# Issuing the first small store between tile 0's activations, and computing the last tile in two chunks of 4 rows

## The chip, the cores and the metric

The kernel runs on one core of a Trainium2 chip. The metric is the device time of one execution in microseconds. Every execution has a trace span too, about 2 us shorter than its time.

## The reference

```python
x: float32 [32, 512, 2048]
x1, x2 = x[..., :1024], x[..., 1024:]
out = x1 * (1 / (1 + exp(-x1))) * x2        # float32 [32, 512, 1024]
```

It reads 134.2 MB and writes 67.1 MB, with one activation and one multiply per output element.

## The kernel before

The 16,384 rows are cut into 16 tiles of 128 partitions with K = 8 rows each. A tile's load is 8 MB (64 KB per partition), its store 4 MB (32 KB per partition). There are two input and two output buffers. The activation runs on ScalarE (ACT in the profile), the multiply on VectorE (DVE). Loads are issued by SyncE (SP), stores by ACT; SPq and ACTq mark the instructions that issue them. Tile 0 and the last tile are computed in chunks of 2 rows, the others in one piece. Tile 0 is stored in five transfers of growing size.

```python
K = 8; KC_EDGE = 2; KS = 4
OPENING = [
    (slice(0, None, 4), slice(0, 2)),      # 256 KB: every 4th partition, rows 0 and 1
    (slice(2, None, 4), slice(0, 4)),      # 512 KB
    (slice(2, None, 4), slice(4, None)),   # 512 KB
    (slice(0, None, 4), slice(2, None)),   # 768 KB
    (slice(1, None, 2), slice(None)),      # 2 MB
]
...
load(0); load(1)
for i in range(n_tiles):
    ...
    if i < n_tiles - 1:
        kc = KC_EDGE if i == 0 else K
        for c in range(0, K, kc):
            silu(ot, xt, c, c + kc)        # ACT
            mul(ot, xt, c, c + kc)         # DVE, in place on ot
        for ps, ks in OPENING if i == 0 else [(slice(None), slice(None))]:
            nc.scalar.dma_start(out=ov[ps, ks], in_=ot[ps, ks])
        if i + 2 < n_tiles:
            load(i + 2)                    # waits until the multiply has freed the input buffer
        continue
    for c in range(0, K, KC_EDGE):         # the last tile
        silu(ot, xt, c, c + KC_EDGE)
        if c == K - KC_EDGE:
            nc.scalar.dma_start(out=ov[:, :KS], in_=ot[:, :KS])
        mul(ot, xt, c, c + KC_EDGE)
    nc.scalar.dma_start(out=ov[:, KS:], in_=ot[:, KS:])
```

Of the kernel before, what the change touches and what calls it, by code (L numbers as in the profile page):

```python
# [1 line left out]

# [4 lines left out]


def issue_ahead_of_the_first_barrier(nc):




    head, body = nc.main_func.blocks[:2]
    load = next(ins for ins in body.instructions if type(ins).__name__ == "InstDMACopy")
    at = next(
        j for j, ins in enumerate(head.instructions)
        if ins.engine == load.engine and type(ins).__name__ == "InstDrain"
    )
    body.instructions = [ins for ins in body.instructions if ins.name != load.name]  # L20
    head.instructions = head.instructions[:at] + [load] + head.instructions[at:]


@with_exitstack
def kernel(
    ctx: ExitStack,
    tc: tile.TileContext,
    x: bass.AP,
    out: bass.AP,
):  # L30






    nc = tc.nc
    P = nc.NUM_PARTITIONS

    x_flat = x.flatten_outer_dims()  # L40
    out_flat = out.flatten_outer_dims()
    num_rows, in_cols = x_flat.shape
    half = in_cols // 2
    dt = x_flat.dtype

    K = 8
    KC_EDGE = 2
    KS = 4
    OPENING = [
        (slice(0, None, 4), slice(0, 2)),  # L50
        (slice(2, None, 4), slice(0, 4)),
        (slice(2, None, 4), slice(4, None)),
        (slice(0, None, 4), slice(2, None)),
        (slice(1, None, 2), slice(None)),
    ]
    PLAN = [K] * (num_rows // (P * K))

    in_pool = ctx.enter_context(tc.tile_pool(name="in_pool", bufs=2))
    out_pool = ctx.enter_context(tc.tile_pool(name="out_pool", bufs=2))

    plan = []
    row = 0
    for k in PLAN:
        plan.append((row, k))
        row += P * k
    assert row == num_rows
    n_tiles = len(plan)

    def view(flat, i):
        row0, k = plan[i]  # L70
        return flat[row0:row0 + P * k].rearrange("(p k) d -> p k d", k=k)

    nc.at_finalize(issue_ahead_of_the_first_barrier)


    ctx.enter_context(tc.manual_schedule())

    loaded = {}

    def load(i):  # L80
        xt = in_pool.tile([P, K, in_cols], dt, name="xt")
        nc.sync.dma_start(out=xt[:, :plan[i][1], :], in_=view(x_flat, i))
        loaded[i] = xt

    def silu(ot, xt, c, ce):
        nc.scalar.activation(  # L86
            out=ot[:, c:ce, :],
            in_=xt[:, c:ce, :half],
            func=mybir.ActivationFunctionType.Silu,
        )  # L90

    def mul(ot, xt, c, ce):
        nc.vector.tensor_mul(  # L93
            out=ot[:, c:ce, :],
            in0=ot[:, c:ce, :],
            in1=xt[:, c:ce, half:],
        )

    load(0)
    load(1)  # L100
    for i in range(n_tiles):
        xt = loaded.pop(i)
        ov = view(out_flat, i)
        ot = out_pool.tile([P, K, half], dt, name="ot")
        if i < n_tiles - 1:
            kc = KC_EDGE if i == 0 else K
            for c in range(0, K, kc):
                silu(ot, xt, c, c + kc)
                mul(ot, xt, c, c + kc)

            for ps, ks in OPENING if i == 0 else [(slice(None), slice(None))]:
                nc.scalar.dma_start(out=ov[ps, ks], in_=ot[ps, ks])
            if i + 2 < n_tiles:
                load(i + 2)
            continue

        for c in range(0, K, KC_EDGE):
            silu(ot, xt, c, c + KC_EDGE)
            if c == K - KC_EDGE:
                nc.scalar.dma_start(out=ov[:, :KS], in_=ot[:, :KS])  # L120
            mul(ot, xt, c, c + KC_EDGE)
        nc.scalar.dma_start(out=ov[:, KS:], in_=ot[:, KS:])


# [1 line left out]
_INS = ['x']  # L126
_OUTS = [((32, 512, 1024), 'float32')]


# [23 lines left out]
```

## Time and profile before

| | before |
|---|---|
| time, 3 runs before the change was tried | 470.62 us median (470.6 to 472.49) |
| span of the profiled run | 468.5 us |
| DVE, ACT busy | 30%, 24% |
| HBM traffic over the span | 430 GB/s |
| first packet, last landing | 1.00 us, 467.51 us |

The way to read it is to ask when the DMA engines were not busy. Between the first packet and the last landing they practically always are (share 1.00 from 1 to 467 us, at 432 GB/s). Of the busy shares only this one is near 100% (DVE has 30%, ACT 24%), so the time is set by the queue of transfers, and compute matters only where it lets that queue run empty. The prediction below shows the lines.

### The profile page before, as it was taken

The page shows a single profiled execution, that of the slowest core. Times are in us where ns is not written, and L with a number is a line of the kernel's source. Part 1 is how long each engine was busy: PE and PEld are TensorE (multiplying, and loading weights), DVE is VectorE, ACT ScalarE, POOL GpSimd, SP SyncE. Part 2 cuts the span into 40 slices and gives each one's busy share as a digit, 9 for nine tenths or more (in the row PEclk, how much of TensorE's full clock was granted, in tenths as well). Part 3 has the DMA queues.
Part 4 walks back from the last instruction along what each step waited for, and adds up shares of the span by engine and source line. Part 5 has one row for each costly group of instructions (what it writes and reads, how often), then busy time and mean ns, then how long its engine had stood idle before and what let it go on. Part 6 is the DMA issues. An engine that isn't in the chain of part 4 may idle for free.

```text
span 468.5 us, 189 instructions
## 1 busy us (share of the span) xinstructions
DVE 139.5 (30%) x22; ACT 114.3 (24%) x23; POOL 0.2 (0%) x4
## 2 busy tenths in 40 slices
DVE  0070600704207052070510606116060150602551
ACT  1142305005050140601406023060230603206060
POOL 0000000000000000000000000000000000000000
DMA  9999999999999999999999999899999899999998
GB/s 425 397 453 425 448 403 403 492 403 403 448 487 408 403 448 414 481 403 425 425 448 448 403 448 492 358 448 448 431 464 448 380 425 492 403 448 403 448 403 359
DMA packets 4881, 201.34 MB, mean 430 GB/s; under 512 B 592, under 2 KB 592, under 8 KB 592
## 3 DMA queue, kind: packets, MB, share of 16 engines
q1 hardware_dynamic: 2304, 134.22, 66.4%
q10 hardware_dynamic: 2576, 67.11, 33.2%
q14 instruction: 1, 0.01, 0.0%
HBM read 134.22 MB, written 67.11 MB: 430 GB/s over the span
## 4 chain that ended last, share of the span: by engine, by line
DMA 72%; DVE 14%; ACT 11%; DVEq 0%; issue 0%
DMA out_dram<-ot 63%; DVE ot L93 14%; ACT ot L86 11%; DMA xt<-in_x_dram 9%; DVEq L148 0%
## 5 line engine op out<-in xcount | busy, mean ns | idle before, releaser
L93 DVE TENSOR_TENSOR ot<-ot,xt 128x8192 f32<-128x8192 f32 (+1 forms) x22 | 139.5, 6363 | 319.2 <-ACT ot L86 319.2
L86 ACT ACTIVATE ot<-xt 128x8192 f32<-128x8192 f32 (+1 forms) x22 | 113.0, 5163 | 340.1 <-DMA out_dram<-ot 306.1
L86 ACT ACT_TABLE_LOAD x1 | 1.3, 1283 | 0.8 <-PEq L137 0.8
L137 POOL MEMSET const-bfloat16-1.0<- 128x1 bf16 x1 | 0.1, 103 | 0.0
L137 POOL MEMSET const-uint8-127<- 128x1 uint8 x1 | 0.1, 102 | 0.0
L137 POOL MEMSET const-float32-0.0<- 128x1 f32 x1 | 0.1, 100 | 0.2 <-issue 0.2
L137 POOL MEMSET const-float32-1.0<- 128x1 f32 x1 | 0.1, 99 | 0.0
## 6 DMA issues: line engine op xcount, KB each, us to landing
out_dram<-ot ACTq DMA_DIRECT2D x14, 4096.0 KB, 42.2
out_dram<-ot ACTq DMA_DIRECT2D x3, 2048.0 KB, 8.8
out_dram<-ot ACTq DMA_DIRECT2D x2, 512.0 KB, 17.1
out_dram<-ot ACTq DMA_DIRECT2D x1, 768.0 KB, 27.9
xt<-in_x_dram SPq DMA_DIRECT2D x16, 35.1
out_dram<-ot ACTq DMA_DIRECT2D x1, 256.0 KB, 10.8
```

The costliest lines, as they stand in the source:

```text
L86: nc.scalar.activation(out=ot[:, c:ce, :], in_=xt[:, c:ce, :half], func=mybir.ActivationFunctionType.Silu,)
L93: nc.vector.tensor_mul(out=ot[:, c:ce, :], in0=ot[:, c:ce, :], in1=xt[:, c:ce, half:],)
L137: nc = _bacc.Bacc("TRN2", target_bir_lowering=False, num_devices=1)
```

## The change

At the head, the first of the five small stores is meant to go out earlier, from between tile 0's activations rather than behind all four. At the tail, the last tile is computed in two large chunks rather than four small ones, and its two stores stand behind both multiplies, each waiting for its own half only (in the profile after, the first is issued at 457.25, the second multiply ends at 461.55).

```diff
-            for c in range(0, K, kc):
+            parts = list(OPENING) if i == 0 else [(slice(None), slice(None))]
+            for n, c in enumerate(range(0, K, kc)):
                 silu(ot, xt, c, c + kc)
+
+                if n == 1:
+                    ps, ks = parts.pop(0)
+                    nc.scalar.dma_start(out=ov[ps, ks], in_=ot[ps, ks])
                 mul(ot, xt, c, c + kc)
-
-            for ps, ks in OPENING if i == 0 else [(slice(None), slice(None))]:
+            for ps, ks in parts:
                 nc.scalar.dma_start(out=ov[ps, ks], in_=ot[ps, ks])
 ...
-        for c in range(0, K, KC_EDGE):
-            silu(ot, xt, c, c + KC_EDGE)
-            if c == K - KC_EDGE:
-                nc.scalar.dma_start(out=ov[:, :KS], in_=ot[:, :KS])
-            mul(ot, xt, c, c + KC_EDGE)
-        nc.scalar.dma_start(out=ov[:, KS:], in_=ot[:, KS:])
+        for c in range(0, K, KS):
+            silu(ot, xt, c, c + KS)
+            mul(ot, xt, c, c + KS)
+        for c in range(0, K, KS):
+            nc.scalar.dma_start(out=ov[:, c:c + KS], in_=ot[:, c:c + KS])
```

## The prediction

> **What bounds the kernel now.** I read the page first (busy shares and the chain), then the busy time by stretch of the span, then the timeline of the two ends, since the change touches only tile 0 and the last of the 16 tiles. The page:
>
> ```profile
> span 468.5 us, 189 instructions
> DVE 139.5 (30%) x22; ACT 114.3 (24%) x23; POOL 0.2 (0%) x4
> ...
> HBM read 134.22 MB, written 67.11 MB: 430 GB/s over the span
> ...
> DMA 72%; DVE 14%; ACT 11%; DVEq 0%; issue 0%
> ```
>
> No compute engine is busy a third of the time; 72% of the chain that ended last is DMA. The chain also shows 25% of DVE and ACT, which would be misleading: a chain names what released each step, not which resource was full. Whether the DMA engines ever ran dry is told by the stretches (columns: stretch, length, DVE, ACT and POOL busy with counts, clock, DMA share, GB/s):
>
> ```profile
> 0.00:1.00 1.00, 0.00 (x0) 0.23 (x1) 0.20 (x4) 1.00 0.00 0
> 1.00:22.00 21.00, 0.00 (x0) 1.18 (x2) 0.00 (x0) 1.00 1.07 449
> 22.00:44.00 22.00, 8.90 (x4) 7.78 (x5) 0.00 (x0) 1.00 0.98 417
> ...
> 120.00:410.00 290.00, 86.92 (x11) 70.29 (x10) 0.00 (x0) 1.00 1.00 434
> 410.00:448.00 38.00, 9.15 (x2) 7.14 (x2) 0.00 (x0) 1.00 0.99 428
> 448.00:458.00 10.00, 8.17 (x4) 7.20 (x4) 0.00 (x0) 1.00 0.97 419
> 458.00:467.00 9.00, 0.73 (x1) 0.00 (x0) 0.00 (x0) 1.00 0.96 409
> 467.00:468.50 1.50, 0.00 (x0) 0.00 (x0) 0.00 (x0) 1.00 0.00 0
> ```
>
> A packet is counted whole where it starts, so a single short stretch can be off by a packet (the 1.07 is that). The reader is to see that all 16 engines move data from 1.0 us to about 467 us, at both ends too. The kernel is a queue of 201.33 MB: at 434 GB/s of the long stretch that is 463.9 us; add 1.0 us before the first packet and 1.5 us after the last (closing work), and 466.4 of 468.5 us are accounted for. **About 2 us** are all that any reordering can win, 0.4%. The time is some 2.1 us over the span (470.62 against 468.5).
>
> **The two ends.** The timeline (start us, length us, engine, line, operation):
>
> ```profile
> 21.87 5.51 ACT L86 ACTIVATE ot<-xt 128x2048 f32<-128x2048 f32 x3 [19.82 <-DMA xt<-in_x_dram]
> 23.81 8.90 DVE L93 TENSOR_TENSOR ot<-ot,xt 128x2048 f32<-128x2048 f32 x4 [23.81 <-ACT ot L86]
> 26.14 0.56 ACTq L112 DMA_DIRECT2D out_dram<-ot  x1
> 27.29 1.89 ACT L86 ACTIVATE ot<-xt 128x2048 f32<-128x2048 f32 x1
> 28.34 6.23 ACTq L112 DMA_DIRECT2D out_dram<-ot  x4
> ...
> 447.89 7.31 ACT L86 ACTIVATE ot<-xt 128x2048 f32<-128x2048 f32 x4 [17.17 <-DMA out_dram<-ot]
> 449.83 8.90 DVE L93 TENSOR_TENSOR ot<-ot,xt 128x2048 f32<-128x2048 f32 x4 [10.39 <-ACT ot L86]
> 454.36 0.34 ACTq L120 DMA_DIRECT2D out_dram<-ot  x1
> 458.76 0.34 ACTq L122 DMA_DIRECT2D out_dram<-ot  x1
> ```
>
> At the head, the first store stands in the program behind all four activations, yet it was issued at 26.14, before the fourth started at 27.29[...]. The first multiply ran 23.81 to 26.11, so the store left 0.03 us after the data it needs. At the tail, the store of tile 14 (issued 439.47, landed 18.0 us later, at 457.5) is still draining when the last tile's first half is issued at 454.36.
>
> [...] the packet records have tile 15's first 16 KB packets right behind tile 14's last packet on each engine. [...] The rows by shape (1897 ns for 2048, 7029 ns for 8192) give (7029 - 1897)/6144 = 0.835 ns and 186 ns[...].
>
> **Head, step by step.** Removed: nothing. Moved: the 256 KB store, from behind activation 4 to between activation 2 and multiply 2. It depends on multiply 1, as before, so it still can't leave before 26.11: issue at 26.14, gain 0. The cost is new: activation 3 now stands behind it. Before, activation 3 started at 25.49; now ACT's sequencer waits until 26.11, issues for 0.56 us (to 26.70), and activation 3 starts near 26.75, 1.26 us late. It ends at 26.75 + 1.90 = 28.65. Multiply 2 ran until 28.31, so multiply 3 starts at 28.67 instead of 28.23, and multiply 4 with it ends at about 33.2 instead of 32.71: **+0.45 us**. On that end hang stores 3 to 5 and load 2, all issued 0.45 us later. Neither is on the path: load 1 lands only at 43.4, so load 2 queues behind 10 us of transfers, and store 2 (issued 28.34, unchanged, landing 43.6) is ahead of stores 3 to 5 in ACT's queue. What the change buys at the head is 0, what it costs is hidden.
>
> **Tail, step by step.** Removed: two activations and two multiplies of 2048 columns per partition, as four of each become two of 4096. From the shapes, an activation of 4096 takes 186 + 4096 x 0.835 = 3.61 us. For the multiply: (8693 - 2286)/6144 = 1.043 ns and 150 ns, so 150 + 4271 = 4.42 us. With the same start, 447.89: activation 1 ends at 451.50, multiply 1 runs 451.52 to 455.94, activation 2 ends near 455.1, multiply 2 runs to about 460.3. The first-half store is issued at 455.96 instead of 454.36 (**1.6 us later**), the second at 460.35 instead of 458.76 (1.6 us later). The coarser chunk saves a little fixed cost and loses the overlap of ACT and DVE, 1.7 us of fill.
>
> Does that reach the end? Tile 14's last packets end per engine between 456.83 and 457.17 (packet records). Before, the first-half store was there 2.5 us ahead of need. Now it has 0.9 to 1.2 us. From an issue to the first packet, the only measurement on an idle queue is the first load: issued at 0.0, packets from 1.00 to 1.80 us depending on the engine. The same for a store gives first packets at 456.96 to 457.76 against a need at 456.83 to 457.17: a bubble of 0 to 0.9 us, **0.4 us** as an estimate. Then 2 MB takes 8 packets of 0.607 us = 4.86 us per engine, to about 462.3; the second half, issued at 460.35, has its packets ready by 461.4 to 462.2, so no second bubble. Last data then lands at 467.5 + 0.4.
>
> **Sum.** Head 0, steady tiles 0 (their instructions and transfers are the same, and the share is 1.00), tail +0.4: span 468.9, time 470.62 + 0.4 = 471.0 us.
>
> **The rivals.**
> 1. The intent works: the first store starts earlier, so the transfers mix sooner and tile 2 gets its buffer sooner. For: tile 2's activation does wait for stores to land (14 such waits, 306.1 us). Against: the store was not stuck, and the engines are full, so even an earlier store only swaps the order of packets. It would make 470.1 to 470.6; the 2 us not accounted for cap it at 468.6.
> 2. The tail's delay shows in full: 1.6 us later stores end the program 1.6 us later, 472.2. For: nothing else is left to do after them. Against: it needs tile 14's store to have ended before 454.4, and it ends at 457.5, which absorbs 2.5 us less the start-up of a transfer.
> 3. The tail's delay is hidden altogether: start-up for a store that follows on a running queue may be under 0.9 us [...]. Then 470.6, no change. This is nearly as likely as my 0.4.
> 4. The held activation 3 disturbs the steady rhythm. If the 0.45 us late load 2 opened a gap, 471.1 alone, 471.5 with the tail. Against: load 1 has 10 us left at that time.
>
> **Range and chances.** Rivals 1 to 4 span 470.1 to 472.2. The runs of the kernel before alone span 470.6 to 472.49, and a median of few runs could catch such a high one, so the range is 470.1 to 472.3, with its middle above the prediction. A change of over 2% means 9.4 us: faster is ruled out by the 2 us that are there to win (0.005 for what I can't see), slower would need the engines to idle for 9 us, which no step comes near (0.01). Within 2%: 0.985.
>
> **What would show each step right or wrong.** Head: the first store's issue stays at 26.1, with activation 3 near 26.75 instead of 25.49, and the fourth multiply ends near 33.2; an issue well before 26 would refute the working. Load 1 still lands near 43.4, and the steady stretch stays at 434 GB/s. Tail: two activations of 3.6 us and two multiplies of 4.4 us, stores issued 8.1 and 12.5 us after the last tile's first activation, and the DMA share between 456 and 458 us a little lower. The prediction is wrong if the last tile's first activation starts more than 0.5 us off 447.9, or if the span moves by over 1.5 us.

That 434 GB/s is all that the 16 engines can move, which the "about 2 us" presume, is not shown; it is the rate of the 290 us from 120 to 410. That a waiting store holds back what stands behind it on ACT, on which the +0.45 us rest, was an assumption until the profile after showed it (store issued from 26.21 to 26.76, third activation at 26.81). Why a store that stands behind four activations is issued before the fourth starts is not shown. The packet records at the tail, in numbers: on each of the 16 engines tile 15's first 16 KB packet starts 0.002 us after tile 14's last packet ends (456.838 after 456.836 on the first, 457.171 after 457.169 on the last).

## The result and the profile after

The changed kernel took 470.46 us (median of 6 runs, 470.3 to 471.49). The kernel before, in 6 runs (the three above and three beside the changed kernel), took 471.23 us (470.6 to 472.49). The ratio is 0.9984, 95% interval 0.9966 to 1.0002: the same at the 2% mark. Ratios here are the mean time of one kernel's fast runs over the mean of the other's in the same call, so they are not quite the ratio of the medians quoted. Executions over 1.5% slower than the fastest of the same kernel are left out of the means.

The execution that was profiled happens to be the slowest of the six, 471.49 us. From its page:

```profile
span 469.6 us, 185 instructions
DVE 139.4 (30%) x20; ACT 114.2 (24%) x21; POOL 0.2 (0%) x4
...
DMA 72%; DVE 14%; ACT 11%; DVEq 1%; issue 0%
```

There are four instructions fewer, and the shares are those of before. The busy time by stretch (stretch, length, DVE, ACT and POOL busy with counts, clock, DMA share, GB/s):

```profile
120.00:410.00 290.00, 86.92 (x11) 70.29 (x10) 0.00 (x0) 1.00 1.00 434
...
448.00:457.00 9.00, 4.21 (x1) 7.12 (x2) 0.00 (x0) 1.00 0.94 408
457.00:458.00 1.00, 1.00 (x2) 0.00 (x0) 0.00 (x0) 1.00 0.08 33
458.00:459.00 1.00, 1.00 (x1) 0.00 (x0) 0.00 (x0) 1.00 1.19 508
```

The middle is untouched at 434 GB/s. Between 457 and 458 us the DMA engines are nearly empty. That looks like the predicted bubble (a time in which the engines have nothing to move), only larger than the 0.4 us put down for it. The timeline of the two ends (start, length, engine, line, operation):

```profile
21.94 3.71 ACT L86 ACTIVATE ot<-xt 128x2048 f32<-128x2048 f32 x2 [19.89 <-DMA xt<-in_x_dram]
23.88 4.49 DVE L93 TENSOR_TENSOR ot<-ot,xt 128x2048 f32<-128x2048 f32 x2 [23.88 <-ACT ot L86]
26.21 0.55 ACTq L113 DMA_DIRECT2D out_dram<-ot  x1
26.81 1.91 ACT L86 ACTIVATE ot<-xt 128x2048 f32<-128x2048 f32 x1 [1.16 <-DVE ot L93]
28.41 0.48 ACTq L116 DMA_DIRECT2D out_dram<-ot  x1
28.63 1.89 ACT L86 ACTIVATE ot<-xt 128x2048 f32<-128x2048 f32 x1
28.76 4.50 DVE L93 TENSOR_TENSOR ot<-ot,xt 128x2048 f32<-128x2048 f32 x2 [0.38 <-ACT ot L86]
...
449.14 7.12 ACT L86 ACTIVATE ot<-xt 128x4096 f32<-128x4096 f32 x2 [17.20 <-DMA out_dram<-ot]
452.79 8.76 DVE L93 TENSOR_TENSOR ot<-ot,xt 128x4096 f32<-128x4096 f32 x2 [12.12 <-ACT ot L86]
457.25 4.67 ACTq L124 DMA_DIRECT2D out_dram<-ot  x2
```

At the head, the first store leaves at 26.21, which is 4.27 us after the first activation (21.94), exactly as before (26.14 - 21.87). The third activation waits 1.16 us behind it. The fourth multiply ends at 28.76 + 4.50 = 33.26 rather than 32.71.

At the tail, everything begins 1.25 us later than before (449.14 against 447.89), although the middle moves data at the same rate. Each transfer's 16 completion records (592 for 37 transfers in both profiles) show why; they are read here as one for each of the 16 DMA engines. The packet records kept name no engine either; packets are put down to one engine where one starts as another ends, which gives 16 unbroken rows in before. "Lag" here is the last engine's landing less the median engine's (the ninth of the 16 to land):

```
profile            span    lag at load 0   at load 3   at tile 14's store
before             468.5   0.35            0.19        0.11
after              469.6   0.35            1.39        1.37
```

(Load 3 lands at 97 us.) In the profiled run, one of the 16 engines fell behind by 1.1 us between 22 and 70 us and stayed behind. The waits for a full transfer end with it: the last tile's activation starts at 449.14, the last engine's share of the store it waits for lands at 449.12, the median engine's at 447.78. The other fifteen ran dry around 457 us, for 0.75 to 1.21 us. The one that lagged had no gap there and its last packet ended last of all, at 468.19 (the others' at 467.92 to 468.06). So the 1.1 us of extra span is not yet evidence about the change: whether it belongs to it had to be tested.

### The profile page after: what moved, and what is told of

Read it like the earlier page. It is cut to its first block, busy times and chain, and to the rows that moved or that the text cites. A ratio compares the mean times of both kernels' runs of the same rounds, so it can differ in the third digit from the quotient of the medians.

```text
span 469.6 us, 185 instructions
## 1 busy us (share of the span) xinstructions
DVE 139.4 (30%) x20; ACT 114.2 (24%) x21; POOL 0.2 (0%) x4
## 3 DMA queue, kind: packets, MB, share of 16 engines
q1 hardware_dynamic: 2304, 134.22, 66.3%
q10 hardware_dynamic: 2576, 67.11, 33.2%
HBM read 134.22 MB, written 67.11 MB: 429 GB/s over the span
## 4 chain that ended last, share of the span: by engine, by line
DMA 72%; DVE 14%; ACT 11%; DVEq 1%; issue 0%
DMA out_dram<-ot 63%; DVE ot L93 14%; ACT ot L86 11%; DMA xt<-in_x_dram 9%; DVEq L150 1%
## 5 line engine op out<-in xcount | busy, mean ns | idle before, releaser
L93 DVE TENSOR_TENSOR ot<-ot,xt 128x8192 f32<-128x8192 f32 (+2 forms) x20 | 139.4, 6984 | 322.1 <-ACT ot L86 322.1
L86 ACT ACTIVATE ot<-xt 128x8192 f32<-128x8192 f32 (+2 forms) x20 | 112.9, 5661 | 341.3 <-DMA out_dram<-ot 307.1
```

Of the source, the lines that this page charges most:

```text
L86: nc.scalar.activation(out=ot[:, c:ce, :], in_=xt[:, c:ce, :half], func=mybir.ActivationFunctionType.Silu,)
L93: nc.vector.tensor_mul(out=ot[:, c:ce, :], in0=ot[:, c:ce, :], in1=xt[:, c:ce, half:],)
```

## The experiments

There were eleven runs. All outputs are right.

The expectations speak of a "slack theory": a store that is issued later costs nothing as long as its first packets are ready before the queue ahead of it runs out. The time by which they are early is the slack. What a delay exceeds it by is a bubble, and costs its length.

### Each half alone, one chunk, and the change again

`e1_head_only` keeps the changed head with the last tile as before:

```diff
-        for c in range(0, K, KS): ...            # the change's last tile
+        for c in range(0, K, KC_EDGE): ...       # the last tile of before
```

> Only the moved first store; the last tile as before. Slack theory: the first store still leaves at about 26.1 to 26.2, the third activation starts near 26.8 instead of 25.5, the fourth multiply ends 0.5 us later, and none of it reaches the end: ratio to before 0.999 to 1.001. Rival (the head's delay of 0.5 us is carried to the end): ratio 1.001. Rival (the change gains at the head, which would explain the measured 0.9984): ratio 0.998 here and 1.000 in the run with the tail alone.

Measured: 470.72 us (470.65 to 472.04), ratio 1.0000 (0.9985 to 1.0014). The head moved as predicted:

```profile
21.76 3.71 ACT L86 ACTIVATE ot<-xt 128x2048 f32<-128x2048 f32 x2 [19.71 <-DMA xt<-in_x_dram]
...
26.02 0.55 ACTq L113 DMA_DIRECT2D out_dram<-ot  x1
26.63 1.91 ACT L86 ACTIVATE ot<-xt 128x2048 f32<-128x2048 f32 x1 [1.16 <-DVE ot L93]
```

The store leaves 4.26 us after the first activation, the third activation is held, and no effect on the time shows. The interval still holds the rival's 1.001; a larger delay, in `e6_head_hold_more` below, settles that.

`e2_tail_only` keeps the changed last tile with the head as before:

```diff
-            for n, c in enumerate(range(0, K, kc)): ...  # the change's head
+            for c in range(0, K, kc): ...                # the head of before
```

> Only the last tile in two chunks of 4 rows; the head as before. Slack theory with a start-up of 0.85 us (first packets of the first-half store in the profile of the changed kernel, 458.09, less its issue at 457.25): issued 8.1 us after the last tile's first activation, first packets at 8.9, need at 8.9 to 9.3: no bubble where no engine lags, ratio 0.999 to 1.001. Rival (every delay of the last stores shows in full): 1.6 us, ratio 1.0034. Where one engine lags the others by about 1 us in the profile, as one did in the changed kernel's, the others idle for about that long before the first-half store and the span is about 1 us longer, but because the lagging engine ends it.

Measured: 470.37 us (470.21 to 473.82), ratio 1.0005 (0.9981 to 1.0030). Four of six runs lie at 470.21 to 470.37. The full delay's 1.0034 lies outside the interval. In the profiled run (472.2) three engines lag by more than 0.5 us, the last of them by 2.0 us. The fifteen others waited 0.5 to 2.1 us before the first-half store (issued at 457.95, first packets at 458.80):

```profile
457.00:458.80 1.80, 1.80 (x2) 0.00 (x0) 0.00 (x0) 1.00 0.11 46
```

So a lag arises with the old head as well.

`e3_tail_one_chunk` computes the last tile in a single chunk:

```diff
-        for c in range(0, K, KS):
-            silu(ot, xt, c, c + KS)
-            mul(ot, xt, c, c + KS)
+        silu(ot, xt, 0, K)
+        mul(ot, xt, 0, K)
```

> The changed kernel with the last tile in one chunk of 8 rows, two stores as in the change. Both stores are issued 7.03 + 8.69 + 0.04 = 15.8 us after the last tile's first activation. Slack theory: first packets at 16.6 against a need at 8.9 to 9.3 where tile 14's store ends, so a bubble of 7.4 us on all engines, then 9.7 us of data; 7.4 us over before, ratio 1.0157. Rival (delay shows in full, 15.8 - 6.5 = 9.3 us): ratio 1.0198. Rival (full engines hide it): 1.000.

Measured: 477.96 us (477.86 to 479.62, 4 runs), ratio 1.0157 (1.0138 to 1.0176), the slack theory's number; the rival's 1.0198 is outside. The timeline, then two stretches of the same profile:

```profile
449.69 7.03 ACT L86 ACTIVATE ot<-xt 128x8192 f32<-128x8192 f32 x1 [17.20 <-DMA out_dram<-ot]
456.75 8.69 DVE L93 TENSOR_TENSOR ot<-ot,xt 128x8192 f32<-128x8192 f32 x1 [15.54 <-ACT ot L86]
465.48 0.82 ACTq L123 DMA_DIRECT2D out_dram<-ot  x2
```

```profile
457.00:460.00 3.00, 3.00 (x1) 0.00 (x0) 0.00 (x0) 1.00 0.03 11
460.00:466.00 6.00, 5.45 (x1) 0.00 (x0) 0.00 (x0) 1.00 0.00 0
```

The engines stand empty until 0.84 us after the issue (first packets at 466.32). The profiled run is again one with a lagging engine (1.9 us). The three others took 477.86 to 478.00.

`e4_after_again` is the changed kernel unedited.

> The changed kernel once more, unedited, on the chip of the three others. Slack theory: ratio to before 0.998 to 1.001, most runs 470.3 to 470.8, and now and then a run of 471.5 to 472.5 in either kernel, whose profile, if one is caught, shows one of the 16 engines landing its share 0.5 us or more after the others from the first store on. If the change itself made the 1.1 us of the profiled run, all profiles of it have a span near 469.6 and those of before near 468.5.

Measured: 470.44 us (470.21 to 471.35), ratio 0.9993 (0.9978 to 1.0008). This time the profiled run had no lagging engine (0.21 us at tile 14's store), and its span is 468.5. Its last tile and the stretch around the seam:

```profile
448.09 7.12 ACT L86 ACTIVATE ot<-xt 128x4096 f32<-128x4096 f32 x2 [17.19 <-DMA out_dram<-ot]
451.74 8.76 DVE L93 TENSOR_TENSOR ot<-ot,xt 128x4096 f32<-128x4096 f32 x2 [12.11 <-ACT ot L86]
456.19 4.67 ACTq L124 DMA_DIRECT2D out_dram<-ot  x2
```

```profile
448.00:458.00 10.00, 6.26 (x2) 7.12 (x2) 0.00 (x0) 1.00 0.97 419
```

The stretch has the 0.97 and 419 GB/s of before. The store was issued at 456.19, and in the packet records its first packets follow tile 14's last ones, near 457.0, without a gap: with the 0.84 us seen where the queue is empty, they were ready just in time. The 1.1 us of the first profile belong to that execution, not to the change.

### How far slack reaches, and three other questions

`e5_tail_six_two` uses chunks and stores of 6 and 2 rows:

```diff
-        for c in range(0, K, KS):
+        for c, ce in ((0, 6), (6, K)):           # both loops
```

> The changed kernel with the last tile in chunks and stores of 6 and 2 rows, between the change (4 and 4) and the single chunk. The first store is issued 5.32 + 6.56 + 0.05 = 11.9 us after the last tile's first activation, its packets come 0.85 us later at 12.8, tile 14's store runs out at 8.9 to 9.2. Slack theory: a bubble of 3.7 us on all engines, ratio to before 1.007 to 1.008. Rival (delay shows in full against 6.5 us in before: 5.4 us): ratio 1.0115. Rival (only the second store's time counts, and it is ready long before its turn): 1.000.

Measured: 473.99 us (473.91 to 474.1), ratio 1.0065 (1.0053 to 1.0077). The issue in the timeline and the stretch behind it:

```profile
459.89 2.54 ACTq L124 DMA_DIRECT2D out_dram<-ot  x2
```

```profile
457.00:460.00 3.00, 3.00 (x2) 0.00 (x0) 0.00 (x0) 1.00 0.00 0
```

The first packets come at 460.73, again 0.84 us after the issue, after idle gaps of 3.5 to 4.0 us per engine, 3.8 on average. The bubble is close to the predicted 3.7. The ratio lies just under the expected 1.007: the median is only 3.3 us above before's 470.73 of this call, some 0.4 us less than the bubble. Part of the difference stands in the profiles: the median engine's last data packet ends 3.84 us later than in before, the last engine's only 3.65 us, as in before one engine ends 0.27 us behind the median and here 0.08. The rest stays open. The delay-in-full rival (1.0115) is refuted.

`e6_head_hold_more` puts the first store right behind the first multiply, so that three activations wait behind it. The cut is against the changed kernel; the last tile is that of before:

```diff
                 silu(ot, xt, c, c + kc)
-                if n == 1:
+                mul(ot, xt, c, c + kc)
+                if n == 0 and i == 0:
                     ps, ks = parts.pop(0)
                     nc.scalar.dma_start(out=ov[ps, ks], in_=ot[ps, ks])
-                mul(ot, xt, c, c + kc)
```

> The last tile as before; at the head the first store is put right behind the first multiply, so that activations 2, 3 and 4 all stand behind it: activation 2 starts near 26.8 instead of 23.7, the fourth multiply ends near 35.4 instead of 32.7, and load 2 is issued 2.7 us late, six times the delay of the change. Theory (load 1 keeps the engines busy until 43, so the delay is hidden): ratio to before 0.999 to 1.001. Rival (delays at the head reach the end): 2.7 us, 1.0057.

Measured: 470.49 us (470.46 to 470.67, 5 runs), ratio 0.9992 (0.998 to 1.0004).

```profile
26.80 5.51 ACT L86 ACTIVATE ot<-xt 128x2048 f32<-128x2048 f32 x3 [2.96 <-DVE ot L93]
28.74 6.70 DVE L93 TENSOR_TENSOR ot<-ot,xt 128x2048 f32<-128x2048 f32 x3 [2.58 <-ACT ot L86]
35.46 24.04 SPq L82 DMA_DIRECT2D xt<-in_x_dram  x2
```

Load 2 is issued at 35.46 rather than 32.74, 2.7 us late, and the time doesn't move. Tile 1's activation still starts at 43.39, when load 1 has landed. The head's delay is hidden at six times its size.

`e7_one_first_store` is the kernel before with one store of 4 MB for tile 0:

```diff
-    OPENING = [ ...five parts... ]
+    OPENING = [(slice(None), slice(None))]
```

> The kernel before with tile 0 stored by one transfer of 4 MB behind its four multiplies, in place of five growing ones: the first store then leaves at about 32.7 instead of 26.1. If an early first store were worth anything, this loses: 6.6 us later, up to 1.014. Theory (the engines are full whichever queue feeds them): no loss, and perhaps a gain, since in the profiles of before and after the load packets that follow the completions of the small stores (near 36, 51 and 60 us) take 2.5 to 2.9 us instead of 2.42, together 0.6 to 0.9 us per engine: ratio 0.998 to 1.000. If the lagging engine of the slower runs is born at these small stores, its runs of 471.3 us and more become rarer too.

Measured: 471.24 us (471.1 to 472.09), ratio 1.0011 (0.9998 to 1.0023). The expected gain did not come, and runs above 471.3 us became no rarer (three of six). The lowest of six runs is 471.1, while most runs of before in that call lie at 470.3 to 470.8. Its timeline:

```profile
450.71 7.31 ACT L80 ACTIVATE ot<-xt 128x2048 f32<-128x2048 f32 x4 [21.93 <-DMA xt<-in_x_dram]
...
457.18 0.34 ACTq L114 DMA_DIRECT2D out_dram<-ot  x1
```

The last tile now waits for its load, which lands at 450.6, and no longer for a store at 447.9. In before that load had landed at 445.4, so it is 5.2 us later; the last tile starts 2.8 us later. (The expectation of `e10_one_first_store_fine_tail` takes the 2.8 us for the load.) Tile 14's store still runs out near 457, so the first-half store, issued at 457.18, comes too late. The engines idle for 0.5 to 1.3 us. The amount of data is the same (134.22 MB read, 67.11 MB written); only its order over the two queues has changed. Nor did the load packets get quicker: those of 64 KB near 36 us took 2.6 to 2.8 us in before, against 2.42 us in the steady part, and 3.2 to 3.5 us here. So the small stores alone are not the cause of the slow packets, which stays open.

`e8_head_two_chunks` is the kernel before with tile 0 in two chunks of 4 rows. It was meant to test a small thing in the profiles: kernels with 189 instructions have one packet of 8 KB in the queue that the page lists as "q14 instruction" (called the fetch here) in the span, during the last store (at 463.60 in before), and those with 185 have none there. (All of them have one after the end of the span, at 470.33 in before and 470.19 in the changed kernel's first profile.)

```diff
-            kc = KC_EDGE if i == 0 else K
+            kc = KS if i == 0 else K
```

> The kernel before with tile 0 in two chunks of 4 rows, the last tile untouched: 185 instructions as in the changed kernel, instead of 189. In the profiles with 189 instructions an instruction fetch of 8 KB falls into the last store (at 463.1 and 463.6) and holds one engine for 0.3 us; in those with 185 it comes after the last store. Fetch theory: no fetch inside the last store here either, last landing even over the engines (last engine within 0.25 us of the median), ratio 0.9993 to 0.9997. Rival (the 0.2 us of the changed kernel come from the form of its last tile): fetch or not, ratio 1.000.

Measured: 472.1 us (470.78 to 483.7), ratio 1.0028 (0.9997 to 1.0059). There is no fetch inside the last store (the only one is at 469.5, after the end), but nothing was gained: the best runs are 470.78 to 470.99. This head also changes the order of the transfers (load 1 lands at 42.3 rather than 43.4, the last tile starts at 448.65), and the engines end up to 0.6 us apart. The run doesn't isolate the fetch and is inconclusive on it.

### The fetch, and the mechanism of the one first store

`e9_after_padded` is the changed kernel with four tiny instructions in the idle 20 us before tile 0:

```diff
     load(0)
     load(1)
+    for j in range(2):
+        nc.vector.memset(pad[:, j:j + 1], 0.0)
+        nc.scalar.activation(out=pad[:, j:j + 1], in_=pad[:, j:j + 1], func=Silu)
```

> The changed kernel with two activations and two memsets of one element per partition before tile 0, in the 20 us in which both engines wait for the first load: 189 instructions again, the ends as in the change. Fetch theory: the instruction fetch falls back into the last store (near 463) and one engine ends 0.3 us after the others; fast runs at 470.5 to 470.7 as before, 0.2 us over those of the changed kernel in this call. Rival (the 0.2 us come from elsewhere in the change, or are chance): fetch or not, the fast runs stay with those of the changed kernel, 470.2 to 470.4.

Measured: 471.02 us (470.81 to 474.46), ratio 0.9994 (0.9958 to 1.0031); the kernel before had runs of up to 475.11. Five of the six runs lie at 470.81 to 471.09. The DMA queues of its profile between 458 and 468 us (queue: packets, MB, share of the engines' time):

```profile
q10 hardware_dynamic: 256, 3.67, 86.9%
q14 instruction: 1, 0.01, 0.2%
```

The q14 line is the fetch, back inside the last store. The kernel before has such a line in the same stretch; the changed kernel, in the control below, has none. The fetch's packet takes 0.31 us on one engine, at 465.86, and the last engine lands its share 0.74 us behind the median. The times fit neither side of the expectation: the narrow group lies above the 470.5 to 470.7 of the fetch theory too.

`e10_one_first_store_fine_tail` has the head of `e7_one_first_store` and stores the last tile in four stores of 2 rows:

```diff
-            if c == K - KC_EDGE:
-                nc.scalar.dma_start(out=ov[:, :KS], in_=ot[:, :KS])
             mul(ot, xt, c, c + KC_EDGE)
-        nc.scalar.dma_start(out=ov[:, KS:], in_=ot[:, KS:])
+        for c in range(0, K, KC_EDGE):
+            nc.scalar.dma_start(out=ov[:, c:c + KC_EDGE], in_=ot[:, c:c + KC_EDGE])
```

> The run with one first store lost 0.6 us; in its profile load 15 lands at 450.7, 2.8 us later than before, tile 14's store still runs out near 457, and the first-half store, issued at 457.18, leaves the engines idle for 0.5 to 1.3 us. Here the same head, but the last tile is stored in four stores of 2 rows, the first of which is issued 4.2 us after the last tile's first activation, near 455.0. Slack theory: its packets come at 455.8, before 457, no bubble, and the loss is undone: ratio to before 0.999 to 1.000, most runs 470.2 to 470.6. Rival (the one first store itself costs 0.6 us at the head): stays at 1.001, 471.1.

Measured: 471.18 us (470.41 to 471.6), ratio 0.9985 (0.9953 to 1.0016). Three runs lie at 470.41 to 470.84, below all six of `e7_one_first_store`, and three at 471.5 to 471.6. The profiled one (471.6) has a lagging engine (1.2 us) but no idle gap on any engine at the seam, even so:

```profile
451.77 5.51 ACT L80 ACTIVATE ot<-xt 128x2048 f32<-128x2048 f32 x3 [21.89 <-DMA xt<-in_x_dram]
...
456.04 0.34 ACTq L115 DMA_DIRECT2D out_dram<-ot  x1
```

The first store leaves 4.3 us after the first activation rather than 6.5 us, in time before 457. That the finer tail closes the bubble is shown. That the bubble was the loss is supported by the three lower runs, but not settled: only one of six runs lies in the expected 470.2 to 470.6, and the two runs compared are from different chips.

`e11_after_control` is the changed kernel again, as control.

> The changed kernel unedited, as the control of the two others on their chip: ratio to before 0.998 to 1.000, fast runs 470.2 to 470.5.

Measured: 471.44 us (470.26 to 473.12), ratio 0.9999 (0.9961 to 1.0036). Its profiled run (470.32) has no fetch within the last store and a lag of 0.37 us. Between tile 14's store and the first-half store at least nine engines idle, none by more than 0.3 us, 1.1 us in all. Only two of its six runs lie in the expected 470.2 to 470.5. 5 of 11 runs of before were above 471.2 too.

### The runs taken together

The times of one kernel fall into a narrow group near its best and a tail of higher ones. I cut at 471.2 us, a value chosen after seeing them, and the chips are mixed.

| kernel | runs | at or below 471.2 | median of these | fetch in the last store |
|---|---|---|---|---|
| before | 39 | 25 | 470.58 | yes |
| `e1_head_only` | 6 | 5 | 470.71 | yes |
| `e6_head_hold_more` | 5 | 5 | 470.49 | yes |
| after | 18 | 13 | 470.37 | no |
| `e2_tail_only` | 6 | 4 | 470.31 | no |
| `e8_head_two_chunks` | 6 | 3 | 470.79 | no |
| `e9_after_padded` | 6 | 5 | 470.99 | yes |

The high runs come to 14 of 39 for before and 5 of 18 for after. Where such a run was profiled (the first profile of the changed kernel, `e2_tail_only`, `e3_tail_one_chunk` by its own scale, `e10_one_first_store_fine_tail`), the last engine lagged by 1.2 to 2.0 us at tile 14's store. No profile within the narrow groups has more than 0.45 us at tile 14's store. In `e2_tail_only` the lag is there in full by 40 us, in the changed kernel it builds up until 70 us, and in the other two it grows over 150 us and more. It comes with the five small stores and with the single one, with the old head and the new. What starts it stays open.

## Why the prediction was right or wrong

The predicted 471.0 lies 0.5 us above the measured 470.46, well within the range, and "within 2%" was right. By its steps:

- **What bounds the kernel** was right. The lowest run of any version is 470.21 us, that of before 470.29, against the 2 us put down as all there was to win. Load 2 issued 2.7 us late cost nothing.
- **Head** was right in every number: issue 4.27 us after the first activation in both kernels, third activation at 26.81 for 26.75, fourth multiply ending at 33.26 for 33.2, effect on the time none (`e1_head_only` 1.0000; `e6_head_hold_more`, with six times the delay, 0.9992). The first store had not been stuck behind the activations, so moving it could not free it.
- **Tail, durations** were right: activations of 3.62 and 3.60 us for 3.61, multiplies of 4.43 and 4.42 for 4.42, stores issued 8.1 and 12.4 us after the first activation for 8.1 and 12.5.
- **Tail, the bubble of 0.4 us** was mis-sized. The failing term is "the same for a store gives first packets at 456.96 to 457.76", which took the start-up of the very first load, 1.00 to 1.80 us, for that of a store. Five profiles in which the queue was empty show 0.84 or 0.85 us from a store's issue to its first packets (457.25 to 458.09, 459.89 to 460.73, 465.48 to 466.32 in three of them), and up to 0.99 us on the slowest engine. That is counted from the start of the issuing instruction, which takes 0.34 us for these stores. With 0.9 to 1.2 us of slack the bubble is 0 (`e4_after_again`) to at most 0.3 us on some engines (`e11_after_control`). Rival 3, the hidden delay, which the prediction called nearly as likely, is what happened; with 0.84 us in the same sum, `e3_tail_one_chunk` was forecast at 1.0157 and came out so.
- **The sign of the sum.** The prediction had +0.4 us; the narrow groups show -0.2 us (470.37 against 470.58). Much of that lies outside what the prediction worked out. Spans (to 0.1 us) for 22 of before's 25 narrow runs and for all 13 of the change's average 468.57 and 468.55 us, while the time less the span averages 2.02 and 1.92 us. Of the 0.12 us between the mean times of these runs, 0.10 us is outside the span. The candidate tested was the fetch. In the four profiles with 189 instructions (before, `e1_head_only`, `e6_head_hold_more`, `e9_after_padded`) one fetch falls into the last store, at 463.1 to 465.9, takes 0.31 us on one engine, and that engine ends last; a second one follows the end of the span, at 470.3 to 470.8. The profiles of the change and of its tail alone have only the second. Yet before's last landing, 467.51, is no later than the 467.53 of `e4_after_again`; `e6_head_hold_more` has the fetch and a narrow group of 470.49; `e8_head_two_chunks` lost it without gaining; and the padded kernel's 0.6 us over its control is twice the packet's 0.31 us. So the fetch is not shown to be the cause. In a pooled comparison, 0.2 us is at the edge of what these runs resolve, and its cause stays open.
- **Luck.** All the prediction's rivals ended between 470.1 and 472.2 us, so a time within its range says little about which working was right. The steps above had to be checked one by one.
- **The signs named in advance.** The last tile's first activation was to lie within 0.5 us of 447.9. In the first profile it was at 449.14, which looked like a refutation, but the two other profiles of the same kernel have 448.09 and 448.01: one lagging engine in one execution. The prediction took the spread of before (to 472.49) into its range without asking what made it.
- **Rival 1's side remark**, that an earlier store "only swaps the order of packets", was too careless. `e7_one_first_store` only swaps the order, and lost about half a microsecond: the last load landed 5.2 us later and the last tile started 2.8 us later, which left its compute with too little store traffic to hide behind. (The ratio's interval, 0.9998 to 1.0023, just includes no loss.)

## What to carry to other kernels

In this kernel, whose transfers fill the DMA engines (share 1.00 from 1 to 467 us), an instruction issued later cost nothing until its transfer missed the moment at which the queue ran empty. For another kernel of this kind work out, at each end, when the queue ahead runs out, when the next store can be issued, and measure the start-up between issue and first packet (0.84 us here). What lay beyond that slack cost nearly its full excess (7.3 of 7.4 us with one chunk of 8 rows, 3.3 of 3.7 us with 6 and 2), and what lay within it cost nothing that these runs resolve (ratio 0.9993 with stores 1.6 us later at the tail, 0.9992 with load 2 issued 2.7 us later at the head). Before a difference of 1 us in one profile is put down to an edit, profile the same kernel again and compare the completions engine by engine.
